# A hybrid RetNet/HGRN2 layer on one core: the diagonal's column sums moved 38 ticks later, the closing norms spread, the sums of activations reordered, and the feed-forward's PSUM pool split in two

## The chip, the cores and the metric

The kernel runs on one core of a Trainium2 chip. The metric is the device time of one execution in microseconds (us). The engines are named as the profile names them: PE is TensorE (matmuls; PEld is its weight load), DVE is VectorE, ACT is ScalarE, POOL is GpSimd and SP is SyncE, whose queue issues nearly all DMAs. "Granted clock" or PEclk is the share of TensorE's full clock that the throttle granted.

## The reference

One inference step of a one-layer decoder for 2048 prompt tokens and 64 sample tokens (8 sequences of 8 tokens), model width 1024. The same weights serve both.

```
hp = rmsnorm(xp, norm_mix_w)
proj = h @ w_in                        # 1024 x 4096: rq rk rv rg hq hf hi hg
rq, rk = rotary(rq), rotary(rk) * dk**-0.5
o_r = chunk_gla(rq, rk, rv, log_gamma) # RetNet: 4 heads, scalar decay per head
f = lb + (1 - lb) * sigmoid(hf)
o_h = chunk_gla(silu(hq) * dk**-0.5, 1 - f, hi, log f)   # HGRN2: 4 heads, decay per channel
o = concat(head_rmsnorm(o_r) * silu(rg), head_rmsnorm(o_h) * silu(hg))
xp = xp + o @ w_out                    # 1024 x 1024
xp = xp + square(relu(rmsnorm(xp) @ w_up)) @ w_down      # 1024 x 4096 x 1024
y = rmsnorm(xp, final_norm_w)
```

`chunk_gla` is S_t = diag(g_t) S_{t-1} + k_t v_t, o_t = q_t S_t, in chunks. Everything is float32; the final states of all heads are outputs too.

## The kernel before, in words

All activations lie feature-major (128 features on the partitions, tokens along the row). Tokens are worked in three groups of 640, 768 and 704 tokens, so a matmul's row is half a group: 320, 384 or 352 wide. Every float32 operand is split into a rounded high part and the remaining low part (`lo`, line 285 for weights; 351 or 1270 for activations), and each product is three matmuls: high by high, high by low, low by high. ACT makes the high part (lines 270, 350, 1266) and DVE or POOL the low part, so each operand passes ACT and then DVE before PE can use it.

The program is mix(g0), out_proj(g0), mix(g1), out_proj(g1), mix(g2), out_proj(g2), then ffn(g0), ffn(g1), ffn(g2). In the trace the mixing takes 0 to about 1220 us and the three feed-forwards begin at about 1221, 1625 and 2097 us.

**What sets the order.** PE's stream of large matmuls (projections at lines 343 and 718; feed-forward at line 1175) is written in program order. `tick` is called after every two of these matmuls (three in the values' projection). Everything else is put on an agenda with `later(n, fn)` or, in `mixer`, `at(n, fn)`: it is issued n ticks on. A tick is a place in the program and not a time; each engine then runs its own queue in order and waits for what it needs.

**mixer**, called once per pair of heads and group, puts on the agenda the score matrices of both heads. The HGRN2 score matrix is built from blocks that halve (64, 32, 16, ... wide): for each width POOL makes two decayed products (lines 860, 861), ACT an exponential (865), DVE two products (871, 872); PE then multiplies (884 for "corners", 941 for the narrower ones) into a bank of the pool `pm`, and DVE copies the result under a mask into the matrix AT (885, 928). The diagonal itself is a column sum: `own_products` multiplies k by q on POOL (891), `own_parts` splits it (ACT 350, DVE 351), `own` sums it over the partitions with a matrix of ones on PE (495 for the high part, 496 for the low part), and DVE copies it under a mask into AT (905). RetNet's scores are PE line 998, read by DVE at 999.

**PSUM.** There are eight banks. In the mixing `pm` has four single banks for the small results, taken in turn, and `pj` two tiles of two banks for the projections. A tile that takes a bank waits until the earlier tile's last reader is done: so line 998, fifth in turn after the diagonal's two sums, waits for line 905. After out_proj(g2) both pools are closed and one pool of four two-bank tiles serves the feed-forward.

**out_proj** first accumulates three quarters of the output projection for all eight blocks of rows (`residual`, line 1191 adds x), then the last quarter per block (line 1235 on DVE, which reads the `pj` tile). `cut_heads` splits the gated head outputs for it.

**Feed-forward.** Up and down projections use a seven-product scheme for 2 x 2 blocks. T1 to T4 are sums and differences of activation blocks B11 to B22 (`plan_operands` loads the blocks and places the sums, DVE line 1277, and their splits, ACT 1266 and DVE 1270, for the two halves v = 0, 1 of the features). `up_two` does the first two tiles with a special order: first the products that need blocks alone, then T2, T3, T1, T4. Products are read from PSUM by DVE at 1394 (first two tiles), 1452 (other up tiles) and 1524 (down). `finish` of a group runs inside the next group's feed-forward: squares, the split of their sum (1345), two small column sums on PE (1353) and the scaling and storing of y (1631).

## Time and profile before

| | |
|---|---|
| median of 3 runs | 2544.09 us (2542.85, 2544.09, 2547.46) |
| the profiled execution | 2547.37 us |
| its span | 2545.6 us |
| mean granted TensorE clock | 0.995 |
| PE busy | 2505.3 us |
| DVE busy | 1859.8 us |
| ACT busy | 1244.7 us |
| POOL busy | 753.7 us |
| moved by DMA | 533.79 MB, mean 210 GB/s |

The page gives busy time, groups of instructions and DMA queues of one profiled execution. Two views more are used: the table of waits, which adds up for each engine and line how long it stood idle and for whom, and a table of windows, which for a stretch of time gives each engine's busy time, the granted clock and the share of the DMA engines. In a timeline each row is a start, a length, the engine, its line and operation, and in brackets the idle time ahead of it with what ended it. Matmuls are pipelined, so their lengths overlap: the step from one start to the next is what a matmul costs.

### The profile page before, as it was taken

Reading aid. Unit: us, or ns where it says so; the run is one execution under the profiler, and the core shown is the slowest. Engines: PE = TensorE matmul, PEld = TensorE weight load, DVE = VectorE, ACT = ScalarE, POOL = GpSimd, SP = SyncE. Lnnn points to the kernel's source line nnn. Section 1 sums busy time; section 2 is a strip of 40 time slices with the busy share of each in tenths; the row PEclk is TensorE's granted clock in tenths of the full one; section 3 lists DMA queues with packets and bytes.
Section 4 is the critical chain, followed back from the end, with each engine's and each line's share of the span. In section 5 each row is a group of like instructions: output and inputs, shape, how many; then the busy total and the mean of one; then the engine's idle time right before and its main releaser. Section 6 shows DMA issues by size and latency. Waiting matters only on the chain.

```text
span 2545.6 us, 41669 instructions
## 1 busy us (share of the span) xinstructions
PE 2505.3 (98%) x16569; PEld 2481.2 (97%) x16569; DVE 1859.8 (73%) x2293; ACT 1244.7 (49%) x1666; POOL 753.7 (30%) x446
## 2 busy tenths in 40 slices
PE   8999999999999999999999999999999999999998
PEld 8999999999999999999999999999999999999998
DVE  6667865657684667786674899685589878668997
ACT  6565653444454444443554555444354436445544
POOL 5223304324311442340222333323233222323321
PEclk9999999999999999999999999999999999999999
DMA  6444583464577466658776756566575545856552
GB/s 245 181 174 174 201 291 135 158 224 162 175 261 253 165 216 231 234 214 294 284 248 202 282 199 215 178 222 218 185 273 184 183 152 193 280 191 240 198 186 88
DMA packets 191378, 533.79 MB, mean 210 GB/s; under 512 B 18896, under 2 KB 60112, under 8 KB 191184
## 3 DMA queue, kind: packets, MB, share of 16 engines
q1 hardware_dynamic: 191040, 531.12, 60.1%
q8 instruction: 130, 2.13, 0.3%
q14 instruction: 64, 0.52, 0.1%
q10 hardware_dynamic: 144, 0.02, 0.0%
HBM read 393.70 MB, written 136.58 MB: 208 GB/s over the span
## 4 chain that ended last, share of the span: by engine, by line
PE 81%; DVE 10%; issue 4%; ACT 3%; POOL 2%; DMA 1%; DVEq 0%; SPq 0%; ACTq 0%; POOLq 0%
PE pj L343 25%; PE pu L1175 22%; PE pd L1175 21%; PE pjv L718 4%; DVE slab L1270 2%; PE mm L884 1%; DVE lo L285 1%; PE po L1064 1%; PE mm L1072 1%; DVE slab L1277 1%; PE po L1066 1%; POOL slab L861 1%; DVE slab L1524 1%; POOL slab L860 1%; DVE slab L872 1%
## 5 line engine op out<-in xcount | busy, mean ns | idle before, releaser
L343 PE MATMUL pj<-slab,hi 128*128 128x320 f32 (+2 forms) x3072 | 662.3, 330 | 9.5 <-ACT hi L270 6.8
L285 POOL TENSOR_TENSOR lo<-raw,hi 128x1024 fp32r<-128x1024 f32 x142 | 380.1, 2676 | 965.7 <-ACT hi L270 810.8
L1175 PE MATMUL pu<-slab,hi 128*128 128x320 f32 (+2 forms) x2688 | 643.5, 323 | 3.9 <-ACT slab L1266 1.3
L270 ACT CAST hi<-raw 128x1024 fp32r<-128x1024 f32 x384 | 402.5, 1049 | 479.0 <-PE pu L1175 219.3
L1175 PE MATMUL pd<-slab,hi 128*128 128x320 f32 (+2 forms) x2656 | 632.5, 322 | 0.0
L343 PEld LDWEIGHTS pj<-slab,hi 128*128 128x128 f32 x3072 | 510.3, 189 | 12.4 <-ACT hi L270 6.8
L1175 PEld LDWEIGHTS pu<-slab,hi 128*128 128x128 f32 x2688 | 469.9, 189 | 5.3 <-ACT slab L1266 1.6
L1175 PEld LDWEIGHTS pd<-slab,hi 128*128 128x128 f32 x2656 | 463.4, 188 | 0.0
L1175 PE MATMUL pu<-slab,lo 128*128 128x320 f32 (+2 forms) x1344 | 433.7, 323 | 0.0
L1175 PE MATMUL pd<-slab,lo 128*128 128x320 f32 (+2 forms) x1328 | 428.2, 322 | 2.0 <-DVE lo L285 2.0
L343 PE MATMUL pj<-slab,lo 128*128 128x320 f32 (+2 forms) x1536 | 379.2, 328 | 0.0
L285 DVE TENSOR_TENSOR lo<-raw,hi 128x1024 fp32r<-128x1024 f32 x242 | 303.5, 1254 | 92.5 <-ACT hi L270 90.4
L343 PEld LDWEIGHTS pj<-slab,lo 128*128 128x128 f32 x1536 | 263.8, 189 | 0.7 <-DVE lo L285 0.3
L1270 DVE TENSOR_TENSOR slab<-slab 128x640 fp32r<-128x640 f32 (+2 forms) x192 | 228.9, 1207 | 40.7 <-ACT slab L1266 26.2
L1175 PEld LDWEIGHTS pu<-slab,lo 128*128 128x128 f32 x1344 | 253.6, 189 | 0.0
L1175 PEld LDWEIGHTS pd<-slab,lo 128*128 128x128 f32 x1328 | 249.1, 188 | 2.7 <-DVE lo L285 2.5
L1266 ACT CAST slab<-slab 128x640 fp32r<-128x640 f32 (+2 forms) x192 | 147.6, 781 | 194.1 <-DVE slab L1277 144.1
L718 PE MATMUL pjv<-hi,slab 128*128 128x256 f32 x1088 | 210.4, 287 | 0.0
L718 PEld LDWEIGHTS pjv<-hi,slab 128*128 128x128 f32 x1088 | 175.1, 193 | 1.4
L1524 DVE TENSOR_TENSOR slab<-pd,slab 128x640 f32<-128x640 f32 (+2 forms) x166 | 145.6, 882 | 36.6 <-PE pd L1175 36.1
L718 PE MATMUL pjv<-lo,slab 128*128 128x256 f32 x544 | 154.6, 284 | 0.0
L1277 DVE TENSOR_TENSOR slab<-slab 128x640 f32<-128x640 f32 (+2 forms) x96 | 123.2, 1304 | 0.3
(206 smaller groups left out, 3094.6 us busy)
## 6 DMA issues: line engine op xcount, KB each, us to landing
raw<-w SPq DMA_DIRECT2D x256, 512.0 KB, 4.4
slab<-u SPq DMA_DIRECT2D x32, 384.0 KB, 5.7
u<-ld SPq DMA_DIRECT2D x30, 384.0 KB, 4.5
slab<-u SPq DMA_DIRECT2D x32, 352.0 KB, 5.1
u<-ld SPq DMA_DIRECT2D x30, 352.0 KB, 4.5
slab<-u SPq DMA_DIRECT2D x32, 320.0 KB, 5.0
u<-ld SPq DMA_DIRECT2D x30, 320.0 KB, 3.4
ld<-x SPq DMA_DIRECT2D x16, 384.0 KB, 5.0
```

What stands on the lines that cost most here:

```text
L270: self.nc.scalar.copy(hi, raw)
L285: eng.tensor_tensor(out=lo, in0=self.second.pop(j), in1=hi.bitcast(F32), op=ALU.subtract)
L343: self.nc.tensor.matmul(pj[:, i, :T2], w, a[:, c0:c1], start=j == 0 and q == 0, stop=j == n - 1 and q == 2)
L718: nc.tensor.matmul(pj[:, i * 256:(i + 1) * 256], a[:, s:s + C], ww, start=kb == 0 and q == 0, stop=kb == KB - 1 and q == 2)
L860: nc.gpsimd.tensor_tensor(out=D4[:, :, 0, :], in0=mid, in1=B4[:, :, 0, :], op=ALU.subtract)
L861: nc.gpsimd.tensor_tensor(out=D4[:, :, 1, :], in0=B4[:, :, 1, :], in1=mid, op=ALU.subtract)
L872: nc.vector.tensor_tensor(out=Q4[:, :, 1, :], in0=D4[:, :, 1, :], in1=blocks(q, w, a)[:, :, 1, :], op=ALU.mult)
L1175: self.nc.tensor.matmul(*a, **k)
L1266: self.nc.scalar.copy(hi[:, :g.T], B[name][:, :g.T])
L1270: self.nc.vector.tensor_tensor(out=lo[:, :g.T], in0=B[name][:, :g.T], in1=hi.bitcast(F32)[:, :g.T], op=ALU.subtract)
L1277: self.nc.vector.tensor_tensor(out=s[:, :g.T], in0=B[a][:, :g.T], in1=B[b][:, :g.T], op=op)
L1524: nc.vector.tensor_tensor(out=r, in0=ps, in1=r, op=ALU.add)
```

## The change

Six edits, of which none adds or removes an instruction on PE (15,663 in both builds):

1. In `mixer` the diagonal's product moves from tick 2 to 40, its split from 12 to 50, and its two column sums from 32 and 34 to 67 and 70.
2. `cut_heads` of the first three pairs is spread over the last gates (ticks 2, 20, 38), where before two ran at the end of the mixing and one at the start of `residual`.
3. `pj` stays open to the end. In out_proj(g2) the four banks of `pm` are closed right after `residual`, and a new pool `pf` with two two-bank tiles opens on them; `tile2` then gives out pf, pf, pj, pj, ... in turn.
4. `plan_operands` makes T3, T2, T1 of v = 0, then T3, T2, T1 of v = 1, then both T4, 8 ticks apart; before it made T3, T2, T1, T4 of one v and then of the other, 9 apart. The loads of the second half move from ticks 36 to 42 to ticks 20 to 24 and 40, that of the first half's B21 from 6 to 38.
5. In `up_two` an addition on DVE (line 1421) comes after the next product's eviction.
6. `finish` begins at tick 96 for 90, its squares are 10 ticks apart for 6, `out` starts at 200 for 180, and `factor` comes 8 ticks ahead of it for 25; the scaling of the next group's residual moves from 170 to 190.

```diff
     def mm(self, cols=512):
-        if self.pm is None:
-            return self.pj.tile([P, 2, 512], F32, tag="pj", name="pm")[:, 0, :cols]
+        if self.pf is not None:
+            return self.tile2()[:, 0, :cols]
...
+    def tile2(self):
+
+        self.n_tiles += 1
+        if self.n_tiles % 4 in (1, 2):
+            return self.pf.tile([P, 2, 512], F32, tag="pf", name="pf")
+        return self.pj.tile([P, 2, 512], F32, tag="pj", name="pj")
...
-            self.out_proj(gs[2], 3, lambda: self.prepare(gs[0], 12))
-
-            mixing.close()
-            self.pj, self.pm = ctx.enter_context(tc.tile_pool(name="pf", bufs=4, space=bass.MemoryType.PSUM)), None
+
+            def end_of_mixing():
+
+                mixing.close()
+                self.pf = ctx.enter_context(tc.tile_pool(name="pf", bufs=2, space=bass.MemoryType.PSUM))
+
+            self.out_proj(gs[2], 3, lambda: self.prepare(gs[0], 12), end_of_mixing)
             self.ffn(gs[0], lambda: self.prepare(gs[1], 8))
-            self.finish(gs[0], begin=90, pace=6, wait=180, each=8)
-            self.ffn(gs[1], lambda: self.prepare(gs[2], 8), 170)
+            self.finish(gs[0], begin=96, pace=10, wait=200, each=8)
+            self.ffn(gs[1], lambda: self.prepare(gs[2], 8), 190)
...
-        for p in range(H - 2):
-            self.cut_heads(g, p)
+        for p in range(H - 1):
+            self.later(2 + 18 * p, self.cut_heads, g, p)
         self.gates(g, prev)
...
-        at(2, own_products)
-        at(12, own_parts)
-        at(32, own, 0)
-        at(34, own, 1)
+        at(40, own_products)
+        at(50, own_parts)
+        at(67, own, 0)
+        at(70, own, 1)
...
     def residual(self, g, when, beside):
 
-        self.cut_heads(g, H - 2)
...
-        t = 10
+        for j, (name, v) in enumerate([(name, v) for v in range(2) for name in ("T3", "T2", "T1")] + [("T4", 0), ("T4", 1)]):
+            self.later(10 + 8 * j, self.block_sum, g, g.B[v], name)
+            for d, fn in zip((14, 18), self.halve(g, g.B[v], name, g.ops[v])):
+                self.later(d + 8 * j, fn)
         for v in range(2):
-            for name in ("T3", "T2", "T1", "T4"):
-                self.later(t, self.block_sum, g, g.B[v], name)
-                for d, fn in zip((4, 8), self.halve(g, g.B[v], name, g.ops[v])):
-                    self.later(t + d, fn)
-                t += 9
-        for v in range(2):
-            for j, name in enumerate(("B22", "B12", "B11", "B21")):
-                self.later(36 * v + 2 * j, load, v, name)
+            for j, name in enumerate(("B22", "B12", "B11")):
+                self.later(20 * v + 2 * j, load, v, name)
+            self.later(38 + 2 * v, load, v, "B21")
...
     def two_banks(self, g):
-        return self.pj.tile([P, 2, 512], F32, tag="pj", name="pu")[:, :, :g.T // 2]
+        return self.tile2()[:, :, :g.T // 2]
...
             add(u2, b, p1)
-            nc.vector.tensor_tensor(out=x4[:, :T], in0=x4[:, :T], in1=u2[:, :T], op=ALU.add)
             d = self.two_banks(g)
             self.product(g, parts(d), "T3")
             add(u3, d, u2)
+            nc.vector.tensor_tensor(out=x4[:, :T], in0=x4[:, :T], in1=u2[:, :T], op=ALU.add)
...
             def open_banks(A):
-                banks[A] = [self.pj.tile([P, 2, 512], F32, tag="pj", name="pd")[:, :, :T2] for _ in range(2)]
+                banks[A] = [self.two_banks(g) for _ in range(2)]
...
-            self.later(wait - 25 + 2 * h, factor, h)
+            self.later(wait - 8 + 2 * h, factor, h)
```

Three places show how the order moves. In the changed file the lines stand 9 to 12 further down: 871, 905, 928 and 999 are 882, 916, 939 and 1010; 1270 and 1277 are 1281 and 1288; 1345 and 1631 are 1354 and 1640; 343 and 351 are the same.

DVE in mix(g1), one pair of heads, before: the split of the diagonal (351) stands ahead of the block products, and its two copies (905) ahead of the copies of the narrower blocks (928) and of the RetNet scores (999).

```order
L351 TENSOR_TENSOR slab<-slab 128x768
L871 TENSOR_TENSOR slab<-slab 128x6x64
L872 TENSOR_TENSOR slab<-slab 128x6x64
L916 TENSOR_TENSOR slab<-slab 128x384
L871 TENSOR_TENSOR slab<-slab 128x12x32
L872 TENSOR_TENSOR slab<-slab 128x12x32
L490 TENSOR_TENSOR slab<-slab 128x384
L871 TENSOR_TENSOR slab<-slab 128x24x16
L872 TENSOR_TENSOR slab<-slab 128x24x16
L905 COPY_PREDICATED AT_160<-msk,mm 128x384
L905 COPY_PREDICATED AT_161<-msk,mm 128x384
L999 TENSOR_TENSOR slab<-mm,con 128x384
```

The same place in the change:

```order
L882 TENSOR_TENSOR slab<-slab 128x24x16
L883 TENSOR_TENSOR slab<-slab 128x24x16
L1010 TENSOR_TENSOR slab<-mm,con 128x384
L939 COPY_PREDICATED AT_160<-msk,mm 128x192
L939 COPY_PREDICATED AT_161<-msk,mm 128x192
L1010 TENSOR_TENSOR slab<-mm,con 128x384
L351 TENSOR_TENSOR slab<-slab 128x768
L882 TENSOR_TENSOR slab<-slab 128x48x8
L883 TENSOR_TENSOR slab<-slab 128x48x8
L896 COPY_PREDICATED AT_160<-msk,mm 128x384
L882 TENSOR_TENSOR slab<-slab 128x96x4
L883 TENSOR_TENSOR slab<-slab 128x96x4
```

The split and both copies of the diagonal now stand behind the RetNet scores; on PE the two column sums moved behind line 998 in the same way.

DVE at the start of ffn(g0), before. A sum (1277) reads two loaded blocks or an earlier sum, its split (1270) follows; the rows here begin with T2 of v = 0 and its split, then T1, T4 (it reads `slab_12864`, that is T2), and at the end T3 of v = 1:

```order
L1277 TENSOR_TENSOR slab_12864<-slab_12831,ld_12815 128x640
L1270 TENSOR_TENSOR slab_12875<-slab_12864,slab_12874 128x640
L1277 TENSOR_TENSOR slab_12896<-ld_12809,ld_12815 128x640
L1270 TENSOR_TENSOR slab_12907<-slab_12896,slab_12906 128x640
L1277 TENSOR_TENSOR slab_12931<-ld_12821,slab_12864 128x640
L285 TENSOR_TENSOR lo_12975<-raw_12881,hi_12974 128x1024
L1270 TENSOR_TENSOR slab_12949<-slab_12931,slab_12948 128x640
L1277 TENSOR_TENSOR slab_12964<-ld_12918,ld_12935 128x640
```

And in the change:

```order
L1288 TENSOR_TENSOR slab_12859<-slab_12828,ld_12814 128x640
L1281 TENSOR_TENSOR slab_12872<-slab_12859,slab_12871 128x640
L1288 TENSOR_TENSOR slab_12895<-ld_12808,ld_12814 128x640
L285 TENSOR_TENSOR lo_12977<-raw_12884,hi_12976 128x1024
L1281 TENSOR_TENSOR slab_12906<-slab_12895,slab_12905 128x640
L1288 TENSOR_TENSOR slab_12917<-ld_12865,ld_12874 128x640
L285 TENSOR_TENSOR lo_13019<-raw_12926,hi_13018 128x1024
L1281 TENSOR_TENSOR slab_12937<-slab_12917,slab_12936 128x640
```

T3 of v = 1 now follows T1 of v = 0 directly; the sum and the split of T4 are behind all six others.

At the same place on PE, the end of out_proj(g2) in the change. Line 1186 is line 1175 of before, the first feed-forward product:

```order
L343 MATMUL pj<-slab,hi 128x352 x4
L343 MATMUL pj<-slab,lo 128x352 x2
L1186 MATMUL pf<-slab,hi 128x320 x2
L343 MATMUL pj<-slab,hi 128x352 x4
L343 MATMUL pj<-slab,lo 128x352 x2
L343 MATMUL pj<-slab,hi 128x352 x4
```

Before, no row of the feed-forward stands among the projection's rows. The first two feed-forward matmuls are now ahead of the projection's last five blocks of rows, on a bank of `pf`; the other feed-forward matmuls follow the last block as before.

DVE in ffn(g1), where the closing norm of g0 runs, before. 1615 adds the squares, 1345 are the splits of the two halves' sums, 1394 and 1421 belong to `up_two`, 1631 scales y:

```order
L1615 TENSOR_TENSOR slab<-slab 128x640
L1369 SCALAR_TENSOR_TENSOR ld<-ld 128x768
L1394 TENSOR_TENSOR slab<-pu,slab 128x768
L285 TENSOR_TENSOR lo<-raw,hi 128x1024
L1421 TENSOR_TENSOR slab<-slab 128x768
L1345 TENSOR_TENSOR slab<-slab 128x640 x2
L1394 TENSOR_TENSOR slab<-pu,slab 128x768
L285 TENSOR_TENSOR lo<-raw,hi 128x1024
L1631 SCALAR_TENSOR_TENSOR slab<-slab,vec 128x320 x4
```

And in the change:

```order
L1624 TENSOR_TENSOR slab<-slab 128x640 x3
L1403 TENSOR_TENSOR ld<-pj,slab 128x768
L1403 TENSOR_TENSOR slab<-pj,slab 128x768
L285 TENSOR_TENSOR lo<-raw,hi 128x1024
L1354 TENSOR_TENSOR slab<-slab 128x640
L1378 SCALAR_TENSOR_TENSOR slab<-slab 128x768
L1403 TENSOR_TENSOR ld<-pj,slab 128x768
L1354 TENSOR_TENSOR slab<-slab 128x640
L1378 SCALAR_TENSOR_TENSOR ld<-ld 128x768
L285 TENSOR_TENSOR lo<-raw,hi 128x1024
L1461 TENSOR_TENSOR slab<-pf,slab 128x768
L1640 SCALAR_TENSOR_TENSOR slab<-slab,vec 128x320 x10
```

The two splits no longer stand side by side and are behind the last evictions of `up_two`. The sums over them on PE moved further: between the place of the second split and the first of these sums stand about 38 large matmuls, where before there were about 14.

More of the change, by code (lines that the diff above doesn't have):

```diff
@@ L379, in build @@
             self.small = ctx.enter_context(tc.tile_pool(name="small", bufs=2))
+            self.pj = ctx.enter_context(tc.tile_pool(name="pj", bufs=2, space=bass.MemoryType.PSUM))
             mixing = ctx.enter_context(ExitStack())
             self.pm = mixing.enter_context(tc.tile_pool(name="pm", bufs=4, space=bass.MemoryType.PSUM))
-            self.pj = mixing.enter_context(tc.tile_pool(name="pj", bufs=2, space=bass.MemoryType.PSUM))
+            self.pf, self.n_tiles = None, 0
             self.dp = ctx.enter_context(tc.tile_pool(name="dp", bufs=1, space=bass.MemoryType.DRAM))
@@ L445, in build @@
             self.mix(gs[2])
-            self.out_proj(gs[2], 3, lambda: self.prepare(gs[0], 12))
-            mixing.close()
-            self.pj, self.pm = ctx.enter_context(tc.tile_pool(name="pf", bufs=4, space=bass.MemoryType.PSUM)), None
+            def end_of_mixing():
+                mixing.close()
+                self.pf = ctx.enter_context(tc.tile_pool(name="pf", bufs=2, space=bass.MemoryType.PSUM))
+            self.out_proj(gs[2], 3, lambda: self.prepare(gs[0], 12), end_of_mixing)
             self.ffn(gs[0], lambda: self.prepare(gs[1], 8))
-            self.finish(gs[0], begin=90, pace=6, wait=180, each=8)
-            self.ffn(gs[1], lambda: self.prepare(gs[2], 8), 170)
-            self.finish(gs[1], begin=90, pace=6, wait=180, each=8)
-            self.ffn(gs[2], None, 170)
+            self.finish(gs[0], begin=96, pace=10, wait=200, each=8)
+            self.ffn(gs[1], lambda: self.prepare(gs[2], 8), 190)
+            self.finish(gs[1], begin=96, pace=10, wait=200, each=8)
+            self.ffn(gs[2], None, 190)
             nc.sync.dma_start(self.O["ret_p"].rearrange("h d v -> d h v"), self.S[:, :H])
@@ L1225, in plan_sums, with out_proj @@
         self.side = deque(sorted(self.side, key=lambda z: z[0]))
-    def out_proj(self, g, when, beside):
+    def out_proj(self, g, when, beside, between=lambda: None):
         nc, T = self.nc, g.T
         part = self.residual(g, when, beside)
+        between()
         g.res, g.in_ = (self.dp.tile([P, KB, T], F32, name=f"{name}{g.i}") for name in ("res", "in"))
```

## The prediction

> **What bounds the kernel now.** I read the page's busy times first, then PE's table of waits, then windows and timelines around the waits.
>
> ```profile
> span 2545.6 us, 41669 instructions
> PE 2505.3 (98%) x16569; PEld 2481.2 (97%) x16569; DVE 1859.8 (73%) x2293; ACT 1244.7 (49%) x1666; POOL 753.7 (30%) x446
> ```
>
> PE is busy 98% of the span. No edit changes PE's work, so only PE's 40 us of idle time, and the time in which its clock is low, can move. The waits behind that idle time:
>
> ```profile
> PE mm L998 <- DVE AT L905: 8.3, 4, 2.5
> PE pj L343 <- ACT hi L270: 6.8, 1, 6.8
> PE pm L1353 <- DVE slab L1345: 2.9, 3, 1.9
> PE pd L1175 <- DVE lo L285: 2.0, 2, 1.6
> PE pj L343 <- ACT slab L350: 1.9, 2, 1.4
> PE pu L1175 <- ACT slab L1266: 1.3, 1, 1.3
> PE pu L1175 <- DVE slab L1270: 1.2, 1, 1.2
> PE mm L496 <- DVE slab L351: 1.1, 1, 1.1
> PE pu L1175 <- DVE slab L1235: 1.1, 1, 1.1
> PE mm L884 <- DVE slab L872: 0.8, 1, 0.8
> PE mm L884 <- DVE AT L928: 0.5, 1, 0.5
> ```
>
> The columns are total us, times, longest. The 6.8 us is the start of the program, which the change leaves alone. The others are short, but a wait costs more than its own length: after it the clock is low. Windows of 6 us (columns: length, busy time of PE, PEld, DVE, ACT, POOL, then granted clock, DMA share, GB/s), the first around a wait of 1.51 us, the next around the longest L998 wait, then the start of the feed-forward and the closing norm:
>
> ```profile
> 422.00:428.00 6.00, 5.76 (x46) 5.22 (x46) 3.56 (x8) 3.02 (x8) 2.86 (x3) 1.00 0.94 357
> 512.00:518.00 6.00, 4.91 (x26) 4.91 (x26) 3.58 (x8) 2.56 (x6) 1.41 (x2) 0.72 0.99 340
> 1246.00:1252.00 6.00, 4.75 (x20) 4.49 (x19) 3.93 (x4) 1.32 (x2) 0.96 (x1) 0.57 0.99 358
> 1252.00:1258.00 6.00, 6.00 (x38) 6.00 (x37) 4.50 (x5) 2.72 (x3) 0.00 (x0) 0.86 0.31 115
> 1679.00:1685.00 6.00, 5.62 (x24) 5.62 (x25) 5.70 (x9) 2.72 (x5) 0.00 (x0) 0.72 0.50 161
> ```
>
> At 422 the clock stays at 1.00; at the others it falls. What that costs is read from the matmul steps behind the longest wait:
>
> ```profile
> 507.53 0.39 PE L718 MATMUL pjv<-hi,slab 128*128 128x256 f32 x2
> 507.76 0.28 PE L718 MATMUL pjv<-lo,slab 128*128 128x256 f32 x1
> ...
> 513.09 1.65 PE L998 MATMUL mm<-slab 128*128 128x128 f32 x6 [2.46 <-DVE AT L905]
> 514.40 0.56 PE L718 MATMUL pjv<-hi,slab 128*128 128x256 f32 x1
> 515.82 1.15 PE L343 MATMUL pj<-slab,hi 128*128 128x384 f32 x4
> ```
>
> A step of L718 is 0.12 us (two in 0.23). From 514.40 to 515.82 the seven of them that the order has there take 0.20 each, 7 x 0.08 = 0.6 us; L998's six before and L343's after them lie in the same low clock, so I take 1.0 us a fall. 0.6 is the lower bound, the window's 6 x 0.28 = 1.7 the upper. [...]
>
> **Edit 1, the diagonal later.** L998 waits for a bank that the diagonal's copy (L905) frees late:
>
> ```profile
> 501.62 1.59 DVE L351 TENSOR_TENSOR slab<-slab 128x768 fp32r<-128x768 f32 x1
> 512.47 1.04 DVE L905 COPY_PREDICATED AT<-msk,mm 128x384 f32<-128x384 uint8 x2
> ...
> 514.78 0.56 DVE L999 TENSOR_TENSOR slab<-mm,con 128x384 f32<-128x384 f32 x1 [1.27 <-PE mm L998]
> ...
> 523.65 0.60 DVE L885 COPY_PREDICATED AT<-msk,mm 128x384 f32<-128x384 uint8 x1 [4.81 <-issue]
> ```
>
> DVE is nearly always busy ahead of that copy, and the split L351 stands in that queue. The change takes split and copies to behind the RetNet scores, where DVE has 4.81 us free against 1.59 + 1.04 of moved work (bare, the split would push the next copies, L885, 1.6 us back). POOL's product, 1.97 us in its own row, finds a gap too:
>
> ```profile
> 495.57 1.97 POOL L891 TENSOR_TENSOR slab<-slab 128x768 f32<-128x768 f32 x1
> 518.07 1.83 POOL L1003 TENSOR_TENSOR slab<-slab,con 128x768 f32<-128x768 f32 x1 [4.66 <-DVE AT L928]
> ```
>
> If that cover were gone, the 1.97 us would delay the next narrow blocks. The first L998 then finds a free bank; the second waits for the copy of a narrower block (L928), which now follows the block products at once. These end by 512.47, where L905 starts now, or up to 1.59 earlier without the split; 0.56 for a score product and half of 1.04 for the copy give 511.9 to 513.5. PE comes there at about 512.9: 510.63 (513.09 - 2.46), three L998, seven L718 and six other matmuls. So 0 to 0.6 is left; I take 0.25, four times. So 8.3 - 1.0 = 7.3 us, and three clock falls (the 1.51 us wait had none) of 1.0: **-10.3**. Bounds: -6.4 (only four times the 1.59 us taken from the queue) to -13.4 (all of 8.3 and three times 1.7).
>
> The same edit lightens DVE in g0 (L496's 1.1, L884's 0.8 and 0.5): **-2.4**, between 0 and -2.4.
>
> **Edit 2, the cuts spread.** L343 waited 1.9 us for bunched casts (ACT L350). Spread over 48 ticks they lie beside the gates, where ACT is about half busy: **-1.9**, between 0 and -1.9.
>
> **Edits 3 to 5 at the start of ffn(g0).** PE waits for L1235, then twice (L1266 and L1270 in the table) for T2 of the second half:
>
> ```profile
> 1221.04 0.54 PE L1175 MATMUL pu<-slab,hi 128*128 128x320 f32 x2 [1.07 <-DVE slab L1235]
> ...
> 1238.62 0.81 DVE L1277 TENSOR_TENSOR slab<-ld,slab 128x640 f32<-128x640 f32 x1
> 1245.43 2.21 DVE L1270 TENSOR_TENSOR slab<-slab 128x640 fp32r<-128x640 f32 x1 [0.79 <-ACT slab L1266]
> ```
>
> The first feed-forward tile now lies on long-free banks: -1.1. But its two hoisted matmuls turn the order of the banks, and one `pj` tile of the projection takes the bank just written; it waits for L1235's 0.9 us and its signal: +1.1 for the 0.3 us that stood there. T4 of the first half (the sum's 0.81 in the row at 1238, its split at as much, and the 0.79 that DVE stood for ACT) goes out of T2's way: 2.4 us earlier. PE comes 1.1 earlier, so of 1.3 + 1.2 there stay 2.5 + 1.1 - 2.4 = 1.2. The clock there (0.57 and 0.86: at most 6 x 0.43 + 6 x 0.14 = 3.4; I take 2.6, since idle time is in it) does not fall with 1.2 us, as at 422. Before 1.1 + 2.5 + 2.6 + 0.3 = 6.5, then 1.1 + 1.2 + 0.3 for a copy that is waited for = 2.6: **-3.9**. Bounds -6 and -1.5 (the clock still falls). The loads of the second half go some 16 ticks up SP's queue, past weight loads, in a stretch with a DMA share of 0.99; weights are fetched ahead, but this is why -1.5 stands. Edit 5 moves one DVE addition behind an eviction, which comes 0.8 us sooner.
>
> **Edit 6, closing norms.** Split and first sum:
>
> ```profile
> 1678.52 1.55 DVE L1345 TENSOR_TENSOR slab<-slab 128x640 fp32r<-128x640 f32 x2
> 1679.38 0.56 PE L1353 MATMUL pm<-slab,ones_r 128*128 128x320 f32 x2 [1.86 <-DVE slab L1345]
> ```
>
> The split is 1.9 us late. With about 38 matmuls between them for 14, and 0.146 us for the narrowest (25 in 3.66 us below), it gains 3.5 us: 2.9 us of waits go, and one clock fall of 1.0: **-3.9**, between -2 and -4.6.
>
> **Edit 3 in the feed-forward.** With four tiles in turn all but one of the openings found banks whose last matmul was a whole product back. With 2 + 2, fourteen have only 24 or 25 matmuls between. One has a late reader, on the last octet of ffn(g0):
>
> ```profile
> 1570.20 0.31 PE L1175 MATMUL pd<-slab,lo 128*128 128x320 f32 x1
> 1573.86 0.46 PE L1175 MATMUL pd<-slab,hi 128*128 128x320 f32 x2
> ...
> 1571.91 3.03 DVE L1277 TENSOR_TENSOR slab<-slab 128x640 f32<-128x640 f32 x1
> 1574.87 0.81 DVE L1524 TENSOR_TENSOR slab<-pd,slab 128x640 f32<-128x640 f32 x1
> ```
>
> The tile's last matmul is at 1570.20, the next opening comes 25 matmuls on, at the second row, 1573.86; its reader ends at 1575.68: +1.8, near the 1.86 us behind which the clock fell in g1: +1.0. PE's 1.6 us wait for L285 soon after, with the same order on DVE, is then absorbed: -1.6. **+1.3**, between 0 and +3 (DVE 1 us later still). A reader that is in time shows as DVE standing for PE, and both readers do so in most of their rows:
>
> ```profile
> DVE slab L1452 <- PE pu L1175: 46.8, 31, 2.1
> DVE slab L1524 <- PE pd L1175: 36.1, 23, 3.2
> ```
>
> This is why I take one late opening of the fourteen and not more.
>
> **Sum:** -10.3 - 2.4 - 1.9 - 3.9 - 3.9 + 1.3 = -21.1. The profiled execution took 2547.4 us, at the top of the three runs and 3.3 above their median. 2547.4 - 21.1 = 2526.3; less 3.3, 2523.
>
> **Rivals.** *A: the mixing keeps its time.* DVE's backlog is what PE meets, and the wait moves from L905 to L928 and on to the next copies, so edits 1 and 2 bring nothing (14.6 us). For it: DVE is busy without a break up to 513.5. Against: 3.58 of 6 us from 512, and 4.81 free at 519. Then 2523 + 14.6 = 2538.
>
> *B: the split pool makes the feed-forward wait, slower.* If a tile's reader ends later than 25 matmuls (25 x 0.147 = 3.7 us, 4.3 in g1) at all fourteen openings as at the one shown, each costs 1.8 + 1.0: 39 us instead of 2.8, so 2523 + 36 = 2559. It decides from nine late openings on (eight more x 2.8 = 22, over the 21.1). For it: the row with 3.03 us shows DVE slowed beside POOL. Against: the two rows on L1452 and L1524, and 0.8 us for reading a tile. [...]
>
> *C: the new order of the sums doesn't do what it says,* because what T2 waits for is the landing of the loads (share 0.99). Then the start keeps its 6.5 us and adds 1.1: 2523 + 5 = 2528.
>
> **Chances.** My forecast, parts of C in it or not, 0.80; A alone 0.12; B 0.05; something else, no change 0.03. Within 0.2% (5.1 us) is what a measurement of this kernel can't tell from no change. A with its 6 us is on that edge: half of it counts as same. Faster 0.88, same 0.07, slower 0.05. The range: below, all bounds of gain (-13.4 - 2.4 - 1.9 - 6 - 4.6) give -28.3, so 2516; above it takes in A, 2538.
>
> **What would show it.** Right: no row "L998 <- AT L905" in the waits; clock 1.00 behind the RetNet scores of g1; no wait of L1353 over 0.5 us; one wait of near 2 us on L1175's pd for L1524 at the end of ffn(g0); total idle of PE down by some 14 us. Wrong: waits on L928's copies of over 1 us in each pair (A); waits of pf and pj tiles for their evictions in all three feed-forwards (B); T2 waiting for DMA (C).

## The result and the profile after

The changed kernel takes 2524.55 us (median of 4 runs, 2521.42 to 2524.90) against 2544.58 us before (4 runs): a ratio of 0.9917, with a 95% interval of 0.9900 to 0.9935. That is 20 us less; 2523 was predicted, in a range of 2516 to 2538. The profiled execution took 2521.42 us, the shortest of the four.

The page's first lines and PE's table of waits (total us, times, longest) of the changed kernel:

```profile
span 2519.6 us, 41663 instructions
PE 2491.7 (99%) x16569; PEld 2470.7 (98%) x16569; DVE 1851.2 (73%) x2293; ACT 1241.5 (49%) x1666; POOL 755.8 (30%) x446
```

```profile
PE pj L343 <- ACT hi L270: 6.6, 1, 6.6
PE mm L812 <- DVE slab L800: 2.1, 2, 1.6
PE pf L1186 <- DVE slab L1533: 1.8, 1, 1.8
PE pf L1186 <- ACT slab L1409: 1.8, 1, 1.8
PE pf L1186 <- DVE slab L1461: 1.7, 1, 1.7
PE pf L1186 <- DVE slab L1281: 1.5, 1, 1.5
PE mm L567 <- DVE slab L597: 1.5, 1, 1.5
PE pj L343 <- DVE slab L1246: 1.0, 1, 1.0
PE pf L1186 <- POOL lo L285: 0.8, 1, 0.8
```

PE stands idle for 27.9 us (2519.6 - 2491.7) where it was 40.3, so 12.4 us less; some 14 were forecast. The 8.3 us for the diagonal's copies, the 2.9 us of the closing norms and the 1.9 us of the cuts are gone. Four waits of 1 us and more are new: L1533 (the eviction that was foretold), L1409, L1461 and L1246 (the size and place foretold, but not for the reason given, as the runs with edits 2 and 3 show). PE's busy time fell as well, by 13.6 us with the same 16,569 matmuls: its mean granted clock was 0.999, where it was 0.995. The windows that answer to those shown of before, in the order RetNet scores of mix(g1), start of ffn(g0), the late eviction, closing norm:

```profile
504.00:510.00 6.00, 6.00 (x59) 5.35 (x57) 5.09 (x8) 3.53 (x9) 3.85 (x3) 1.00 0.93 297
1217.00:1223.00 6.00, 5.37 (x36) 5.37 (x37) 4.82 (x6) 5.03 (x8) 0.00 (x0) 1.00 0.50 138
1555.00:1561.00 6.00, 6.00 (x41) 6.00 (x42) 4.87 (x6) 4.72 (x6) 0.58 (x1) 1.00 0.62 208
1659.00:1665.00 6.00, 6.00 (x37) 6.00 (x36) 6.00 (x8) 3.94 (x5) 1.18 (x1) 1.00 0.48 171
```

The clock is at 1.00 in all four. DVE's timeline around the RetNet scores (1010) shows why nothing waits there any more:

```profile
504.16 1.26 DVE L883 TENSOR_TENSOR slab<-slab 128x384 f32<-128x384 f32 x1
505.34 0.54 DVE L1010 TENSOR_TENSOR slab<-mm,con 128x384 f32<-128x384 f32 x1
506.50 1.04 DVE L939 COPY_PREDICATED AT<-msk,mm 128x192 f32<-128x192 uint8 x2 [0.62 <-PE mm L507]
507.33 0.59 DVE L1010 TENSOR_TENSOR slab<-mm,con 128x384 f32<-128x384 f32 x1
508.22 1.60 DVE L351 TENSOR_TENSOR slab<-slab 128x768 fp32r<-128x768 f32 x1 [0.29 <-ACT slab L350]
```

DVE waits for PE here (0.62 us ahead of L939) and not PE for DVE. The diagonal's split, 1.60 us, comes behind it all.

### The profile page after: what moved, and what is told of

The parts are those of the page before. It is cut to its first block, busy times and chain, and to the rows that moved or that the text cites. A ratio compares the mean times of both kernels' runs of the same rounds, so it can differ in the third digit from the quotient of the medians.

```text
span 2519.6 us, 41663 instructions
## 1 busy us (share of the span) xinstructions
PE 2491.7 (99%) x16569; PEld 2470.7 (98%) x16569; DVE 1851.2 (73%) x2293; ACT 1241.5 (49%) x1666; POOL 755.8 (30%) x446
## 4 chain that ended last, share of the span: by engine, by line
PE 93%; DVE 5%; issue 1%; ACT 1%; DMA 1%; POOL 0%; DVEq 0%; ACTq 0%; POOLq 0%; SPq 0%
PE pj L343 28%; PE pf L1186 24%; PE pj L1186 23%; PE pjv L729 8%; PE mm L895 2%; DVE slab L1281 1%; PE mm L1083 1%; PE po L1075 1%; PE po L1077 1%; PE mm L952 1%; DVE slab L1288 1%; PE mm L507 1%; PE mm L506 1%; DVE lo L285 1%; PE mm L1009 1%
## 5 line engine op out<-in xcount | busy, mean ns | idle before, releaser
L285 POOL TENSOR_TENSOR lo<-raw,hi 128x1024 fp32r<-128x1024 f32 x142 | 388.9, 2739 | 947.6 <-ACT hi L270 789.7
L343 PE MATMUL pj<-slab,hi 128*128 128x320 f32 (+2 forms) x3072 | 664.6, 329 | 7.6 <-ACT hi L270 6.6
L1186 PE MATMUL pf<-slab,hi 128*128 128x320 f32 (+2 forms) x2768 | 659.2, 322 | 6.8 <-DVE slab L1533 1.8
L270 ACT CAST hi<-raw 128x1024 fp32r<-128x1024 f32 x384 | 402.7, 1049 | 456.7 <-PE pf L1186 179.2
L1186 PE MATMUL pj<-slab,hi 128*128 128x352 f32 (+2 forms) x2608 | 622.1, 322 | 0.2 <-DVE slab L1403 0.2
L343 PEld LDWEIGHTS pj<-slab,hi 128*128 128x128 f32 x3072 | 509.5, 189 | 9.6 <-ACT hi L270 6.6
L1186 PEld LDWEIGHTS pf<-slab,hi 128*128 128x128 f32 x2768 | 481.0, 188 | 8.1 <-issue 2.0
L1186 PEld LDWEIGHTS pj<-slab,hi 128*128 128x128 f32 x2608 | 454.0, 188 | 0.8 <-issue 0.5
L1186 PE MATMUL pf<-slab,lo 128*128 128x320 f32 (+2 forms) x1384 | 445.4, 322 | 0.8 <-POOL lo L285 0.8
L1186 PE MATMUL pj<-slab,lo 128*128 128x352 f32 (+2 forms) x1304 | 420.1, 322 | 0.3 <-DVE lo L285 0.3
L285 DVE TENSOR_TENSOR lo<-raw,hi 128x1024 fp32r<-128x1024 f32 x242 | 303.3, 1253 | 107.4 <-ACT hi L270 99.1
L343 PE MATMUL pj<-slab,lo 128*128 128x320 f32 (+2 forms) x1536 | 379.5, 328 | 0.0
L343 PEld LDWEIGHTS pj<-slab,lo 128*128 128x128 f32 x1536 | 263.8, 189 | 0.8 <-DVE lo L285 0.3
L1186 PEld LDWEIGHTS pf<-slab,lo 128*128 128x128 f32 x1384 | 260.2, 188 | 1.5 <-POOL lo L285 1.2
L1281 DVE TENSOR_TENSOR slab<-slab 128x640 fp32r<-128x640 f32 (+2 forms) x192 | 228.0, 1203 | 40.9 <-ACT slab L1277 26.9
L1186 PEld LDWEIGHTS pj<-slab,lo 128*128 128x128 f32 x1304 | 245.3, 188 | 0.5 <-DVE lo L285 0.5
L876 ACT ACTIVATE slab<-slab 128x640 f32<-128x640 f32 (+2 forms) x72 | 56.3, 782 | 154.0 <-POOL slab L872 153.8
```

The lines of the kernel that those rows point to most:

```text
L270: self.nc.scalar.copy(hi, raw)
L285: eng.tensor_tensor(out=lo, in0=self.second.pop(j), in1=hi.bitcast(F32), op=ALU.subtract)
L343: self.nc.tensor.matmul(pj[:, i, :T2], w, a[:, c0:c1], start=j == 0 and q == 0, stop=j == n - 1 and q == 2)
L876: nc.scalar.activation(x["dd", w][:, a:T], x["dd", w][:, a:T], AF.Exp)
L1186: self.nc.tensor.matmul(*a, **k)
L1281: self.nc.vector.tensor_tensor(out=lo[:, :g.T], in0=B[name][:, :g.T], in1=hi.bitcast(F32)[:, :g.T], op=ALU.subtract)
```

## The experiments

Each run is compared with the kernel before on the same chip, and three chips were used. Before takes 2545.03 us (15 runs) beside edit 1 alone, the column sums, edit 6 alone and the changed kernel again; 2545.24 us (21 runs) beside edit 3 alone, the change without edit 3, edit 4 alone and the scaling of y spread out; 2544.93 us (15 runs) beside edits 1 and 2, edits 4 and 5, the change without edit 6 and the last kernel. The 95% interval of a ratio reaches 2 to 3.5 us either way.

### Edit 1 alone

```diff
-        at(2, own_products)
-        at(12, own_parts)
-        at(32, own, 0)
-        at(34, own, 1)
+        at(40, own_products)
+        at(50, own_parts)
+        at(67, own, 0)
+        at(70, own, 1)
```

> Edit 1 alone (the diagonal's product, split and column sums later), the rest as before. Theory (the bank that the diagonal's late copy frees is what L998 waits for): no wait of L998 for L905 is left, at most 0.3 us each for L928's copies, the clock stays at 1.00 in mix(g1), and of the change's 20 us edit 1 gives 13 to 17: 2528 to 2532. Rival A (the mixing keeps its time, the wait moves on to the next copies): waits of 1 us and more on L928 or L885 in each pair, 2540 or more. The clock terms told apart by the size: with 1.0 us a fall 2532, with 1.7 to 2 us a fall 2529.

Measured: 2529.53 us, ratio 0.9939 (0.9926 to 0.9951), so 15.5 of the 20 us. No wait of L998 is left in its profile. Between the start of the last stretch of mix(g0) and the end of mix(g1) the matmuls come 13.8 us earlier than before (3.4 us earlier at 290 us, 17.2 at 704). 8.3 of these are waits. The other 5.5 us come with the three clock falls behind these waits, some 1.8 us each. In the profile of before each of the three is 3.41 us at 0.50 (from 513.02, 605.18 and 697.34); the mean granted clock of the profiled execution is 0.998 with edit 1 and 0.995 before, and in the changed kernel's profile the clock is 1.00 through the whole mixing. By my estimate from these numbers a fall by itself costs at most half of 3.41, 1.7 us; the few tenths beyond that are not told apart. So theory and large clock term hold, and rival A falls.

### Only the column sums later, the split where it was

```diff
-        at(32, own, 0)
-        at(34, own, 1)
+        at(67, own, 0)
+        at(70, own, 1)
```

> Only the diagonal's two column sums go later (ticks 67 and 70 for 32 and 34); its product on POOL and its split on ACT and DVE stay where they were. Theory (the bank counts, not the load on DVE): the waits of L998 for L905 go as in edit 1, and only the second L998 waits for L928, 0.5 to 1.0 us each since the split's 1.59 us are still ahead in DVE's queue: 2530 to 2535. Rival (DVE's load ahead of the copy is what counts): L998 still waits 1.5 to 2.5 us four times, now for L928, with the clock falling: 2540 to 2544.

Measured: 2533.13 us, ratio 0.9950 (0.9937 to 0.9962). Three rows of its table of waits, the first in out_proj(g2), the others in mix(g0):

```profile
PE pj L343 <- DVE slab L1191: 1.9, 1, 1.9
PE pj L343 <- ACT slab L728: 1.1, 1, 1.1
PE mm L941 <- DVE AT L928: 1.1, 1, 1.1
```

No wait of L998, not even for L928, though the split's 1.59 us are still ahead in DVE's queue (the two copies, 1.04 us, moved with the sums). What PE waited for was the bank that the diagonal held; the rest of DVE's load was not enough to stop it. Moving product and split as well brings the other 3.6 us. Of these, 2.2 are the waits for L728 and L928 in g0, which edit 1 whole doesn't have. The 1.9 us for L1191 at 1195 us is a load of x that landed late; it comes and goes between runs with the same edits there (0.3 us before, 1.9 with edit 6 alone, 0.8 with edit 3 alone), so it isn't put down to an edit.

### Edits 1 and 2

```diff
-        for p in range(H - 2):
-            self.cut_heads(g, p)
+        for p in range(H - 1):
+            self.later(2 + 18 * p, self.cut_heads, g, p)
```

(with edit 1, and without the call of `cut_heads` in `residual`)

> Edits 1 and 2 (the diagonal later, the cuts spread), the rest as before. Theory (the bunched casts hold up PE at the end of a mixing): the waits of L343 for L350's casts, 1.5 us with edit 1 alone, go: 2527 to 2528.5. Rival (they are covered or come back at the next wait): 2529.5.

Measured: 2528.62 us, ratio 0.9934 (0.9922 to 0.9947). The wait of L343 for L350's casts is gone, but out_proj(g2) now waits for its own eviction:

```profile
PE pj L343 <- DVE slab L1234: 1.9, 2, 1.0
```

No such row stands in the table of before or of edit 1 alone. This is the wait of 1.0 us that I had put down to the two hoisted matmuls of edit 3; here nothing is hoisted, so it comes with the cuts. Edit 2 gives 0.8 us (16.3 against 15.5), on two chips and with intervals that overlap, so its size is not resolved: the 1.5 us of casts that edit 1 alone has are gone, and the 1.9 us of the row above came in the next stage.

### Edit 3 alone: the split pool

```diff
+    def tile2(self):
+
+        self.n_tiles += 1
+        if self.n_tiles % 4 in (1, 2):
+            return self.pf.tile([P, 2, 512], F32, tag="pf", name="pf")
+        return self.pj.tile([P, 2, 512], F32, tag="pj", name="pj")
```

(with the pools, `end_of_mixing` and `two_banks` of the change)

> Edits 3 and 5's place alone: pf of two tiles on pm's banks and pj kept, in turn, the rest as before. Theory (the split pool brings one late opening and no more): the wait of 1.1 us at the first feed-forward matmul goes, one of about 1.0 us for L1235's eviction comes inside out_proj(g2), one of 1.8 us comes for L1524's eviction at the end of ffn(g0) and takes the place of the 1.6 us for L285 behind it: 2544 to 2546, no difference. Rival B (the split pool makes the feed-forward wait): waits of 1 to 2 us for evictions in several places of all three feed-forwards, 2550 or more.

Measured: 2544.59 us, ratio 0.9995 (0.9986 to 1.0004): no difference. The one late opening is there, and the wait of 1.6 us for L285 behind it is gone; the one of 1.0 us in the table is elsewhere, at 1487 us. The wait of 1.0 us inside out_proj(g2) that theory and prediction tie to this edit is not there. The two waits for T2 at the start of ffn(g0), 2.5 us, are gone too, though T4 of the first half still stands ahead of T2 of the second; waits for weights, 0.7 us (L270) and 1.1 us (L285 on POOL), came in their place:

```profile
PE pf L1186 <- DVE slab L1536: 1.8, 1, 1.8
PE pj L1186 <- DVE lo L285: 1.2, 2, 1.0
```

### The change without edit 3: one pool of four tiles

```diff
-            self.out_proj(gs[2], 3, lambda: self.prepare(gs[0], 12), end_of_mixing)
+            self.out_proj(gs[2], 3, lambda: self.prepare(gs[0], 12))
+
+            mixing.close()
+            self.pj, self.pm = ctx.enter_context(tc.tile_pool(name="pf", bufs=4, space=bass.MemoryType.PSUM)), None
...
-        return self.tile2()[:, :, :g.T // 2]
+        return self.pj.tile([P, 2, 512], F32, tag="pj", name="pu")[:, :, :g.T // 2]
```

> The changed kernel with one pool of four tiles after out_proj, as before (edit 3 undone, the rest kept). Theory (the split pool is worth nothing either way): the 1.8 us for L1533's eviction goes and the 1.6 us for L285 behind it comes back; the wait of 1.0 us inside out_proj goes and 1.1 us at the first feed-forward matmul comes back: 2523 to 2526. Rival B (the split pool costs): 2521 or less. Rival (the two matmuls hoisted into out_proj are what helps): 2527 or more.

Measured: 2521.58 us, ratio 0.9905 (0.9892 to 0.9919). It is 3.0 us under the changed kernel (2524.54 in its second set of runs). Its four runs lie between 2521.13 and 2522.87, seven of the changed kernel's eight between 2523.87 and 2524.90 and one at 2521.42; the intervals of the two ratios overlap (0.9902 to 0.9929 for the changed kernel). So together with the other edits the split pool costs most likely some 3 us, and not the 36 of rival B with its fourteen late openings. The profiles show only a part of it: PE's idle time is 28.3 us here, 28.7 in the second profile of the changed kernel and 27.9 in the first, so the waits account for little. Clock falls behind the changed kernel's longer waits would fit the rest: the mean granted clock of the four executions here is 0.998 once and 0.999 three times, and of the changed kernel's eight 0.997 twice, 0.998 four times and 0.999 twice. Where the falls of the unprofiled executions lie, no run shows. Its waits in the feed-forward:

```profile
PE pu L1176 <- DVE lo L285: 2.0, 2, 1.6
PE pu L1176 <- DVE slab L1451: 1.8, 1, 1.8
PE pu L1176 <- POOL lo L285: 1.6, 2, 0.8
PE pu L1176 <- DVE slab L1236: 1.1, 1, 1.1
PE pu L1176 <- DVE slab L1271: 0.4, 1, 0.4
```

The eviction's 1.8 us is gone and L285's 1.6 us is back, which is even. The wait inside out_proj(g2) has stayed, against the theory. What differs most is the start of ffn(g0): the wait of 1.1 us for the projection's eviction is back, but the 1.8 us for L1409 and the 1.5 us for T2 (L1281) have shrunk to 0.4 us together. In the changed kernel these two look like this:

```profile
1211.28 1.05 ACT L270 CAST hi<-raw 128x1024 fp32r<-128x1024 f32 x1 [1.89 <-PE pj L1186]
1212.23 0.72 ACT L1277 CAST slab<-slab 128x640 fp32r<-128x640 f32 x1
1216.27 0.72 ACT L1277 CAST slab<-slab 128x640 fp32r<-128x640 f32 x1 [3.31 <-DVE slab L1288]
1216.90 0.69 ACT L1409 COPY slab<-pf 128x640 f32<-128x640 f32 x1
```

```profile
1208.77 0.82 DVE L1288 TENSOR_TENSOR slab<-ld 128x640 f32<-128x640 f32 x1 [6.78 <-DMA ld<-in]
1212.98 2.52 DVE L1281 TENSOR_TENSOR slab<-slab 128x640 fp32r<-128x640 f32 x1 [3.38 <-ACT slab L1277]
1215.42 0.81 DVE L1288 TENSOR_TENSOR slab<-slab,ld 128x640 f32<-128x640 f32 x1
```

The first sum (1208.77) comes when its load has landed. Its split then waits 3.38 us for ACT's cast, because a weight cast (L270) that waits 1.89 us for PE stands ahead of that cast on ACT. The split takes 2.52 us, and only then the sum T2 comes, 6.65 us after the first. ACT's cast of T2 waits 3.31 us for that sum, and the copy L1409, which PE needs for its bank, is queued on ACT behind this cast though its product is ready. With one pool the weight cast stands behind the first sum's cast, and the split waits and takes less:

```profile
1212.93 1.92 DVE L1271 TENSOR_TENSOR slab<-slab 128x640 fp32r<-128x640 f32 x1 [1.60 <-ACT slab L1267]
```

There T2 comes 4.67 us after the first sum (1210.11 to 1214.78). So what delays this chain is the order on ACT, and a split that takes 0.6 us longer, and not the load; why the order came out so with the split pool is open.

### Edit 4 alone, and with edit 5

```diff
+        for j, (name, v) in enumerate([(name, v) for v in range(2) for name in ("T3", "T2", "T1")] + [("T4", 0), ("T4", 1)]):
+            self.later(10 + 8 * j, self.block_sum, g, g.B[v], name)
...
+            add(u3, d, u2)
+            nc.vector.tensor_tensor(out=x4[:, :T], in0=x4[:, :T], in1=u2[:, :T], op=ALU.add)
```

(the last line is edit 5, and stands in the second kernel only)

> Edit 4 alone (T3, T2, T1 of both halves ahead of both T4; loads of the second half earlier). Theory (T4's work stood in T2's way): the two waits of 1.3 and 1.2 us of L1175 at the start of ffn(g0) shrink to one of about 1 us and the low clock behind them does not come: 2541 to 2543.5. Rival C (what counts is when the loads land): both waits stay, 2545.

> Edits 4 and 5 together, the rest as before. Theory (edit 4 frees T2 but what it gains is lost at the next evictions of up_two, for which the addition of edit 5 stood in the way on DVE): no wait of L1175 for T2 over 0.5 us, and none for L1394's evictions over 0.5 us: 2541 to 2543.5. Rival (the evictions are late for another reason): waits of 1 us for L1394 as with edit 4 alone, 2545.

Measured: 2545.45 us (ratio 1.0002, 0.9993 to 1.0011) and 2544.76 us (0.9998, 0.9989 to 1.0007). The edit does what it says: T2's waits, 2.5 us in all, are down to 0.4 us in both profiles. The split of T2's second half ends 16.4 us after the start of the first sum with edit 4 alone, where it was 20.0 before, so the edit frees 3.6 us. In the changed kernel, behind the weight cast shown above, it is 19.7. The time is not kept. Rows of edit 4 alone, then of edits 4 and 5:

```profile
PE pu L1175 <- DVE slab L1392: 2.7, 4, 1.1
PE pu L1175 <- DVE slab L1270: 0.4, 1, 0.4
```

```profile
PE pu L1175 <- DVE slab L1392: 2.1, 2, 1.5
PE pu L1175 <- ACT slab L1308: 1.7, 1, 1.7
PE pu L1175 <- DVE slab L1270: 0.4, 1, 0.4
```

PE arrives sooner at `up_two`'s evictions (1392) and waits there; the 1.5 us for L1392 in the second table is in ffn(g2). The row of 1.7 us names line 1308, which scales the residual; an eviction, which DVE starts at 1256.12 behind a weight split (285), ends within 0.1 us of it, so the wait can be for that. My theory for both runs fell: the evictions are late with edit 5 too, and what makes them late these runs don't settle. One thing more is gone with edits 4 and 5: the waits of the closing norm for its split, 2.9 us before, 1.6 with edit 4 alone, have no row in the table of edits 4 and 5. Rival C had the time right (2545) with the wrong place.

### Edit 6 alone, and the change without it

```diff
-            self.finish(gs[0], begin=90, pace=6, wait=180, each=8)
+            self.finish(gs[0], begin=96, pace=10, wait=200, each=8)
...
-            self.later(wait - 25 + 2 * h, factor, h)
+            self.later(wait - 8 + 2 * h, factor, h)
```

> Edit 6 alone (closing norms later and spread). Theory: the waits of L1353 for L1345 go, 2.9 us with one clock fall, but the scaling of y, bunched behind the factor on DVE, now stands ahead of an eviction of an up product in ffn(g2) and PE waits 1.7 us for it as in the changed kernel: 2540 to 2542.5. Rival (the new wait and its clock fall take it all back): 2544 to 2545.

> The changed kernel with the closing norms as before (edit 6 undone). Theory (edit 6 is worth its 2.9 us of waits and a clock fall, less the wait of 1.4 to 1.7 us that the bunched scaling brings): the waits for the split come back, 2.9 us, the one for L1461 goes: 2526 to 2528.5. Rival (edit 6 is worth nothing, as alone on the kernel before): 2524 to 2525.

Measured: edit 6 alone 2547.19 us, ratio 1.0005 (0.9996 to 1.0014), no gain; the change without it 2527.75 us, ratio 0.9931 (0.9917 to 0.9944), 3.2 us over the changed kernel. Alone it removes the 2.9 us of L1353 as meant, and two others grow:

```profile
PE pd L1175 <- DVE lo L285: 4.1, 6, 1.6
PE pu L1175 <- DVE slab L1452: 2.6, 2, 2.0
```

2.9 us go, and with them the wait of 1.86 us behind which the clock fell before (0.50 from 1680.38 to 1683.79); 2.1 (4.1 for 2.0) and 2.6 come, and the profile's mean granted clock is 0.995 as it was. That is about even: no gain, as the rival says. (The 2547.19 lies 2 us above before, within the interval; a late load of x, 1.9 us for L1191, is in this profile too.) The change without edit 6 waits at two places of ffn(g2) that the change doesn't have:

```profile
PE pj L1186 <- DVE slab L1403: 2.1, 2, 1.5
PE pj L1186 <- ACT slab L1622: 1.1, 1, 1.1
```

The longer of the first row is for an eviction of `up_two`, on DVE right behind a split of the closing norm (1354). Edit 6 removes these and brings the 1.7 us for L1461. The theory's 2526 to 2528.5 has the time right, but not the reason: it lets the 2.9 us of waits for the split come back, and none of them does, since they are gone with edits 4 and 5. That the time fits is luck. What an edit is worth here depends on the others.

### The scaling of y spread out

```diff
-            self.finish(gs[0], begin=96, pace=10, wait=200, each=8)
+            self.finish(gs[0], begin=96, pace=10, wait=204, each=14)
...
-                nc.vector.scalar_tensor_tensor(out=r[:, i], in0=r[:, i], scalar=self.vec[:, V_FIN + n:V_FIN + n + 1],
-                                               in1=x["t", h][:, :T2], op0=ALU.mult, op1=ALU.mult)
+                self.tc.keep_in_program_order(nc.vector.scalar_tensor_tensor(
+                    out=r[:, i], in0=r[:, i], scalar=self.vec[:, V_FIN + n:V_FIN + n + 1],
+                    in1=x["t", h][:, :T2], op0=ALU.mult, op1=ALU.mult))
```

The new wait for L1461 in the changed kernel, DVE first:

```profile
2137.88 6.20 DVE L1640 SCALAR_TENSOR_TENSOR slab<-slab,vec 128x384 f32<-128x384 f32 x9
2144.00 1.22 DVE L285 TENSOR_TENSOR lo<-raw,hi 128x1024 fp32r<-128x1024 f32 x1
2145.14 3.83 DVE L1640 SCALAR_TENSOR_TENSOR slab<-slab,vec 128x384 f32<-128x384 f32 x3
2148.88 0.88 DVE L1461 TENSOR_TENSOR slab<-pf,slab 128x704 f32<-128x704 f32 x1
```

```profile
2149.82 0.59 PE L1186 MATMUL pf<-slab,hi 128*128 128x352 f32 x2 [1.69 <-DVE slab L1461]
```

Twelve scalings and a split hold DVE for 11 us ahead of the eviction. The agenda's distance between them, 8 ticks, has no say in this: built with 16 ticks the program has the same order on DVE, and with the 14 of the edit above but without its hold there are still bunches of 8 and 7 (neither was run). Holding them to their place in the program spreads them.

> The changed kernel with the scaling of y held to its place on the agenda, one step each 14 ticks, so that it stands between the evictions on DVE and not in bunches of 9 and 10 ahead of one. Theory (the wait of 1.4 to 1.7 us of L1186 for L1461 in ffn(g2) comes from the bunch ahead of it on DVE): that wait goes, 2522.5 to 2523.5. Rival (it comes from the two-tile pool): the wait stays, 2524.5.

Measured: 2523.40 us, ratio 0.9911 (0.9898 to 0.9925). The wait for L1461 is gone from its table. The gain of 1.1 us over the changed kernel is what the wait suggests, though the single runs (2521.35 to 2525.41) overlap with that one's.

### One pool and spread scaling

The edits of the two kernels above together.

> The changed kernel with one pool of four tiles in the feed-forward and the scaling of y held between the evictions, one step each 14 ticks. Theory (both costs are real and apart): neither the wait for L1533's eviction nor the one for L1461's, 2519.5 to 2520.8. Rival (the time that the spread scaling saves comes back elsewhere): 2521.6 as with one pool alone.

Measured: 2519.57 us (2517.42 to 2521.23), ratio 0.9898 (0.9885 to 0.9912): 25.4 us less than before and 5.0 us less than the change. It has neither wait; its longest rows behind the start of the program are:

```profile
PE mm L802 <- DVE slab L790: 2.1, 2, 1.6
PE pu L1176 <- DVE lo L285: 1.9, 2, 1.6
PE pj L343 <- DVE slab L1236: 1.7, 2, 1.0
```

### The changed kernel again

> The changed kernel once more, for a second profile. Theory (the clock falls behind some of the waits of 1.5 to 1.8 us and not behind others, by chance of when they come): 2524.5, with the granted clock at 0.997 to 0.999, and where it is under 0.999, a low clock for 3.4 us behind one or two of the waits of L1186. Rival (the clock follows the length of the wait alone): the same waits, of the same length, have 1.00 behind them in every profile, and the 3.5 us between executions come from somewhere else.

Measured: 2524.54 us. The waits are the same to a hundredth of a microsecond at most places, but the clock is not. Windows behind the waits for the copy (1.76 us, at 1218) and the late eviction (1.79 us, at 1556), of this run:

```profile
1218.00:1224.00 6.00, 5.40 (x37) 5.40 (x38) 4.84 (x6) 5.03 (x8) 0.00 (x0) 1.00 0.50 140
1556.00:1562.00 6.00, 6.00 (x30) 6.00 (x31) 4.08 (x5) 4.54 (x6) 0.00 (x0) 0.72 0.66 210
```

and of the kernel with spread scaling, which has the same two waits:

```profile
1218.00:1224.00 6.00, 5.36 (x26) 5.37 (x27) 4.26 (x5) 3.49 (x6) 0.00 (x0) 0.72 0.51 135
1558.00:1564.00 6.00, 5.86 (x40) 5.89 (x41) 5.01 (x6) 4.72 (x6) 0.45 (x1) 1.00 0.66 216
```

In the first profile of the change, with 1.00 in both windows behind its waits of 1.76 and 1.80 us, neither fell; in these two one each, and not the same one. So in these three profiles the length of the wait alone doesn't set the clock.

## Why the prediction came out right

The total, -21.1 us by the sum and -20.0 measured, is right, but in part by luck: the term of edit 1 was 2.8 us too small, the other three together 3.5 us too large, and they cancel:

| step | predicted | measured, and how |
|---|---|---|
| edit 1, in g1 and g0 | -10.3 - 2.4 | -15.5 (edit 1 alone) |
| edit 2 | -1.9 | -0.8 (edits 1 and 2, less edit 1) |
| edits 3 to 5 | -3.9 + 1.3 | -0.9 (change without edit 6, less edits 1 and 2) |
| edit 6 | -3.9 | -3.2 (change, less change without edit 6); 0 alone |
| sum | -21.1 | -20.4 |

The right column takes differences of runs on different chips, and its rows of 0.8 and 0.9 us lie within the intervals.

**Edit 1.** The mechanism was right: the bank, and the free stretch on DVE behind the RetNet scores. The mis-sized terms are the clock fall, 1.0 us predicted and some 1.8 measured, about the upper bound of 1.7 that I had from the window, and the 1.0 us left for L928, which is 0. I counted the slow steps of L718 and left out most of what else ran in the same 3.41 us at 0.50 (513.02 to 516.43). Against it, the waits of mix(g2) grew from 1.0 to 2.1 us (L801, 812 in the change), which no step of mine had.

**Edits 3 to 5.** The eviction foretold is there to the tenth, 1.8 us for L1533, with L285's 1.6 us absorbed behind it. The 1.0 us for L1246 inside out_proj(g2) is there too, but the step that gave it, the hoisted matmuls that turn the order of the banks, is wrong: it comes with edit 2. The step that failed is "T4 goes out of T2's way: 2.4 us earlier". By itself edit 4 does so, by 3.6 us, but in the change the split of T2's second half ends only 0.3 us earlier after the first sum than before (19.7 for 20.0): a weight cast that waits for PE holds up the first sum's cast on ACT, and two splits take 2.5 us each. PE, 1.1 us early, met this and the copy queued behind T2's cast: 1.8 + 1.5 us in place of my 1.2 + 0.3. Rival C, T2 waiting for its load, is not it: the load has landed 3.5 us before ACT's cast of the first sum begins. The clock term of +1.0 for the eviction came in some executions only: behind that wait of 1.8 us the clock is 0.72 over 6 us in the second profile of the changed kernel, and 1.00 in the first and in the one with spread scaling.

**Edit 6** gave 3.2 of 3.9 us, but not by the step in the sum. The 2.9 us of waits of L1353 are in the profile with edits 1 and 2 and not in the change without edit 6, so the other edits had taken them away already; edit 6 removed 2.6 us of other waits in ffn(g2) and brought 1.7 us by the bunched scaling ahead of an eviction. That makes 0.9 of the 3.2 us, and the rest is not shown. Neither was in the sum: it followed the split's way to PE and not what else moves on DVE.

**Rivals.** A is excluded by edit 1 alone, where no wait moves on to the next copies. B, in the form of fourteen late openings, did not come: one was late. But the split pool is a loss of some 3 us beside the other edits, where I had 1.3 (1.1 gained and 1.1 lost at the start, 1.3 lost later).

## What to carry to other kernels

Here, where PE is busy 98% of the time, a wait of PE was worth its length and, where the clock fell behind it, the low clock as well: 8.3 us of waits with three falls gave 13.8 us. Look for the tile whose bank is handed on, not for the engine that is busiest. Where a chain passes from engine to engine, freeing one of them is not enough: edit 4 by itself freed 3.6 us on DVE and in the change 0.3, where a weight cast stood in the chain's way on ACT. Ask for each freed microsecond what its engine meets next, and time edits together, since the closing norms were worth 0 alone and 3 us beside the rest. Where a scheduler orders an engine's queue, a distance in the program need not spread work on that engine; here holding the instructions to program order did.

## What the runs showed of the hardware

In the profile of before the granted clock is 0.50 in five places ahead of the program's end: for 3.41 us from 513.02, 605.18, 697.34 and 1680.38, and for 6.82 us from 1246.89. Between them it is 1.00. PE's waits at these places, and its other waits from 1.3 us on behind the start of the program, where the clock stays at 1.00:

| wait of PE, us | ends at, us | clock at its end or just behind it |
|---|---|---|
| 2.46 (L998) | 513.09 | 0.50 for 3.41 us |
| 2.46 (L998) | 605.47 | 0.50 for 3.41 us |
| 1.83 (L998) | 697.12 | 0.50 for 3.41 us |
| 1.86 (L1353) | 1679.38 | 0.50 for 3.41 us |
| 1.30 and 1.25 (L1175) | 1245.45 and 1247.69 | 0.50 for 6.82 us |
| 1.64 (L1175) | 1600.60 | 1.00 |
| 1.51 (L998) | 422.24 | 1.00 |
| 1.49 (L556) | 28.29 | 1.00 |
| 1.37 (L343) | 1147.89 | 1.00 |

In the first profile of the change the clock is 1.00 up to 2516.30, where PE's work is done, also behind waits of 1.80 us (1555.00), 1.76 (1217.63) and 1.69 (2149.82). Other executions have a fall behind a wait of the same length at the same place: 0.72 over 1556 to 1562 us in the changed kernel's second profile, and over 1218 to 1224 us with spread scaling and in the change without edit 6. The wait of 1.9 us for the closing norm's split has 1.00 behind it with edit 1 alone (1662 to 1668 us) and 0.72 with edits 1 and 2 (1661 to 1667 us). So behind 2.46 us it fell both times, behind 1.7 to 1.9 us in some executions and not in others, and behind 1.3 us where two waits end 2.24 us apart. What sorts these was not shown, and no run varied a wait by itself.

Executions of one kernel with nearly the same waits can differ by this. The profiled execution of the change, 2521.42 us, had no fall between its start and the end of PE's work. The second, 2523.87 us, had the one at 1556 us, at most 1.7 us by the estimate above, and 0.9 us more of waits for L1246.
